# A transformer trunk on one core: transposed input loaded, a quarter of one modulation on TensorE, and a new order of the first loads

## The chip, the cores and the metric

The kernel runs on one core of a Trainium2 chip. The metric is the device time of one execution in microseconds. Three runs of the kernel before took 1611.92, 1613.42 and 1616.47 us; their median is 1613.42 us. The engines of the core are TensorE (PE in the profile; PEld are its weight loads), VectorE (DVE), ScalarE (ACT), GpSimd (POOL) and SyncE (SP), which here only issues transfers. All arithmetic is in 32 bits.

## The reference

One encoder layer over 256 tokens of width D = 2048, with a condition vector c that modulates it:

```python
cond = silu(c)
sh1, sc1, g1, sh2, sc2, g2 = split(cond @ ada_w + ada_b, 6)      # 2048 each
h = rmsnorm(x, norm1_g) * (1 + sc1) + sh1
x = x + g1 * mixer(h)       # q, k, v, u = split(h @ w_in); neighbourhood attention of 16 heads,
                            # a 2-D Fourier mix of u, a sigmoid gate per branch (h @ w_bg), output projection
h = rmsnorm(x, norm2_g) * (1 + sc2) + sh2
x = x + g2 * hier_moe(h)    # one of 4 groups, then 2 of its 8 SwiGLU experts, per token
out = rmsnorm(x, final_g)
```

The weights of all 32 experts (2 MB tiles, 403 MB in all) are read whatever the routing; with the other weights some 611 MB come from memory in each execution. The change concerns sh1 and sc1 (shift 1 and scale 1), the normalised x that they are applied to, and the first products with w_in and w_bg.

## The kernel before

**Layout.** The modulated input h is kept transposed: 16 chunks of 128 channels (on the partitions) by 256 tokens, each as a sum of a high part `hh` and a low part `hl` in a rounded 32-bit type. A *pair* is two neighbouring chunks; there are 8 pairs. Every weight tile is [128, 1024] (512 KB). `load` (L100) takes the next of `NW` = 8 buffers in turn and issues the transfer on SP's queue, which therefore holds the tiles in the order of the program and stops where a buffer is not free yet. `split_w` (L110) makes the high part of a weight tile on ScalarE (L107) and the low part on VectorE (L108). `t_part` and `n_part` multiply one weight tile (512 output columns, two chunks) in 24 matmuls of 256 columns, or 12 of 512: high by high, high by low, low by high.

**The start.** ScalarE's queue brings c, the constant table, a table of vectors and x (tokens on the partitions, two tiles of 1 MB). The silu of c is made twice: as `condR`, its row broadcast to all partitions by matmuls with a row of ones (L190 to L197), and as `condT`, transposed (L198 to L201). The sums of squares of x are made on ScalarE (L339), `rstd_of` makes the reciprocal root, VectorE scales x (L342), TensorE transposes it in 32 pieces (L348), and ScalarE and VectorE copy them to `xT` (L350).

**Shift 1 and scale 1.** `ada1_some(n)` (L238) takes the next n of 64 weight tiles, eight for each pair. Each holds, for 128 output channels on the partitions, half of the 2048 inputs along the row. `dot` (L213) multiplies it by `condR` on VectorE and sums along the row. After the eighth, `h_pair` (L247) makes shift and scale (`modulation`, L225), applies them to two chunks of `xT` (VectorE L252, ScalarE L253), and splits the result into `hh` and `hl`.

**The first loop (L356 to L379).** Its four passes p = 0 to 3 cover the 16 chunks, four chunks (two pairs) in a pass, for nine sections of 512 output columns, listed in `first`: u twice, q, k, v and four gate sections. A pass has 18 loads, two per section (s = 0 needs the first pair, s = 1 the second). The two u sections (si < 2) keep their sums in PSUM over all passes; the others are evicted at the end of each pass: by ScalarE (L377) in pass 0, by VectorE as an addition to the tile in SBUF (L379) later. In a pass the loads of the first four sections are ordered s = 0 of all four, then s = 1; the five others follow one by one. After each load, `want` says how many of the 64 tiles of shift 1 and scale 1 are to have been used by then; `LEAD` = 3 sets them ahead. When none is left, `ada_some(1)` starts on the tiles of the other modulations (128 tiles in all, multiplied and accumulated on VectorE, L223, `mac`), one for each load, also in all later sections up to the output projection; there `PACE` gives 14 more, and the rest are taken after it.

**Order.** The program is written in this order, and a planner that works on modelled times orders the instructions of each engine, with the program's order as priority. `keep_in_program_order`, which the change uses, pins an instruction behind the instruction that the program wrote last on the same engine.

**After the loop** come the Fourier mix, attention, the branch projections, the output projection, routing, and from about 680 us on the experts, whose weights stream through SP's queue.

Of the kernel before, what the change touches and what calls it, by code (L numbers as in the profile page):

```python
# [15 lines left out]
P = 128  # L16
# [41 lines left out]
def build(tc, A, out, dbg=None):  # L58
# [106 lines left out]
    c16 = cp.tile([16, P], F32, name="c16")  # L165
# [7 lines left out]
    nc.scalar.dma_start(c16, A["c"])  # L173
# [15 lines left out]

    condR = xp.tile([P, D], F32, name="condR")  # L190
    for i in range(2):
        crow = wp.tile([P, 1024], F32, tag="w", name=nm("crow"))
        nc.sync.dma_start(crow[0:1, :], A["c"].rearrange("a b -> (a b)")[None, 1024 * i:1024 * i + 1024])
        for j in range(2):
            ps = acc.tile([P, 512], F32, tag="acc", name=nm("pc"))
            mm(ps, ones[0:1, :], crow[0:1, 512 * j:512 * j + 512], True, True)
            nc.scalar.activation(condR[:, 1024 * i + 512 * j:1024 * i + 512 * j + 512], ps, AF.Silu)  # L197
    nc.scalar.activation(c16, c16, AF.Silu)  # L198
    pt = mps()
    nc.tensor.transpose(pt[:, :16], c16, ident[:16, :16])  # L200
    nc.vector.tensor_copy(condT, pt[:, :16])  # L201
# [23 lines left out]
    def modulation(dst, parts, k, vs, vc, vn):  # L225

        bi = [vecT[:, v + k.start:v + k.stop] for v in (vs, vc, vn)]
        nc.vector.tensor_tensor(dst, parts[:, :, :, 0], parts[:, :, :, 1], op=OP.add)
        nc.vector.tensor_tensor(dst[:, 0], dst[:, 0], bi[0], op=OP.add)
        nc.vector.scalar_tensor_tensor(dst[:, 1], dst[:, 1], 1.0, bi[1], op0=OP.add, op1=OP.add)  # L230
        nc.vector.tensor_tensor(dst[:, 1], dst[:, 1], bi[2], op=OP.mult)

# [14 lines left out]
    def h_pair(pr):  # L247
# [3 lines left out]
        hf = s4([P, 2, T], "hf")  # L251
        nc.vector.tensor_scalar(hf[:, 0, :], xT[:, 2 * pr, :], ab[:, 1, 0:1], ab[:, 0, 0:1], op0=OP.mult, op1=OP.add)  # L252
# [83 lines left out]
    xT = xp.tile([P, KC, T], F32, name="xT")  # L336
    xTv = xT.rearrange("p k t -> p (k t)")
# [5 lines left out]
    for k2 in range(8):  # L343
        px = acc.tile([P, 512], F32, tag="acc", name=nm("px"))
        for i in range(2):
            for tb in range(2):
                kc = 2 * k2 + i
                nc.tensor.transpose(px[:, T * i + P * tb:T * i + P * tb + P], xt[tb][:, kc * P:kc * P + P], ident)  # L348
        pv = px.rearrange("p (a b) -> p a b", a=2)
# [3 lines left out]
    at_u, mp_u = att.tile([P, 2, 512], F32, tag="s", name="at_u"), [mps(), mps()]  # L353
    fixed = [[x.rearrange("p (a b) -> p a b", a=2) for x in v] for v in ((at_u[:, 0], at_u[:, 1]), mp_u)]
# [635 lines left out]
```

## Time and profile before

| | |
|---|---|
| median of three runs | 1613.42 us |
| the profiled execution's own time | 1614.69 us |
| its span (first to last instruction) | 1612.9 us |
| busy: PE, DVE, ACT, POOL | 1236.5, 680.5, 349.5, 45.1 us |
| bytes moved, mean rate | 616.27 MB, 382 GB/s |
| mean granted clock of TensorE | 0.901 |

The profile comes from one execution. Busy time is a sum over instructions of an engine; matmuls are pipelined, so that a busy TensorE need not be at its peak. A wait is put down to what ended last of those things that an instruction waited for. The chain of waits follows the work that ended last back from the end. A few per cent of the matmul records can be missing.

### The profile page before, as it was taken

To read this page: it belongs to the slowest core of one execution; us is meant where nothing else is said; L and a number is where in the kernel's file an instruction comes from. 1 tells how busy PE (TensorE), PEld (TensorE's weight loads), DVE (VectorE), ACT (ScalarE), POOL (GpSimd) and SP (SyncE) were. 2 spreads that over 40 slices of the span, in tenths; PEclk is the share of its full clock that TensorE was granted. 3 is DMA by queue.
4 is the path that set the end of the run, shared out by engine and by line. 5 is a ranking of instruction groups with operands and counts; after the bars stand their busy time and mean duration, and the time that the engine had idled before them with its cause. 6 is when DMAs were issued, how large, how long until landed. Compare 5 with 4: busy or idle time off the path is not lost.

```text
span 1612.9 us, 20394 instructions
## 1 busy us (share of the span) xinstructions
PE 1236.5 (77%) x8430; PEld 749.7 (46%) x8430; DVE 680.5 (42%) x946; ACT 349.5 (22%) x535; POOL 45.1 (3%) x40
## 2 busy tenths in 40 slices
PE   5999999999999869798658558558568567555765
PEld 3989899898899746544103113113113012111111
DVE  6989999788887936712002002002003002002002
ACT  4543355444545324211001001000000000000001
POOL 0000000300001100000000000000000000000001
PEclk9999999999999989899789889889859779778878
DMA  9999999899997997699999999999999999999996
GB/s 361 388 334 348 352 341 363 277 327 376 315 352 259 337 407 265 245 402 427 427 426 426 427 427 427 426 427 427 427 427 426 427 428 427 417 426 427 424 427 283
DMA packets 89228, 616.27 MB, mean 382 GB/s; under 512 B 10036, under 2 KB 10340, under 8 KB 64936
## 3 DMA queue, kind: packets, MB, share of 16 engines
q1 hardware_dynamic: 87700, 611.10, 94.5%
q10 hardware_dynamic: 1252, 3.48, 0.6%
q8 instruction: 68, 1.11, 0.3%
q0 software_dynamic: 176, 0.31, 0.1%
q14 instruction: 32, 0.26, 0.0%
HBM read 611.71 MB, written 2.10 MB: 381 GB/s over the span
## 4 chain that ended last, share of the span: by engine, by line
DMA 48%; PE 32%; DVE 6%; issue 2%; ACT 1%; DVEq 0%; ACTq 0%; SPq 0%
DMA w<-exw 43%; PE acc L116 16%; DMA w<-ada 3%; PE ph L116 3%; PE pu L116 3%; PE pg L116 3%; PE pd L116 3%; DVE lo L108 2%; PE m L116 2%; DVE ada L223 2%; DMA w<-mow 1%; PE po L116 1%; PE pr L116 1%; ACT hq L755 0%; DMA w<-mixw 0%
## 5 line engine op out<-in xcount | busy, mean ns | idle before, releaser
L116 PE MATMUL pg<-w,hq 128*32 128x512 f32 x1024 | 179.9, 754 | 222.6 <-DMA w<-exw 222.6
L108 DVE TENSOR_TENSOR lo<-w,hi 128x1024 fp32r<-128x1024 f32 x192 | 239.4, 1251 | 45.4 <-ACT hi L107 39.3
L107 ACT CAST hi<-w 128x1024 fp32r<-128x1024 f32 x192 | 200.7, 1050 | 246.3 <-PE acc L116 170.7
L788 DVE TENSOR_TENSOR act<-act,pu 128x512 f32<-128x512 f32 x8 | 5.5, 688 | 524.0 <-PE pu L116 524.0
L116 PE MATMUL acc<-hh,hi 128*128 128x256 f32 x768 | 211.2, 279 | 0.6 <-ACT hi L107 0.6
L116 PE MATMUL acc<-hl,hi 128*128 128x256 f32 x768 | 210.5, 277 | 0.0
L116 PE MATMUL acc<-hh,lo 128*128 128x256 f32 x768 | 205.1, 278 | 3.0 <-DVE lo L108 3.0
L116 PEld LDWEIGHTS pg<-w,hq 128*32 128x32 f32 x1024 | 24.6, 116 | 364.5 <-DMA w<-exw 345.7
L116 PE MATMUL pu<-w,hq 128*32 128x512 f32 x1024 | 187.6, 782 | 0.0
L223 DVE SCALAR_TENSOR_TENSOR ada<-w,condT,ada 128x1024 f32<-128x1024 f32 x124 | 163.4, 1323 | 34.1 <-DMA w<-ada 33.1
L116 PE MATMUL pd<-w,aT 128*32 128x512 f32 x1024 | 137.7, 656 | 31.9 <-DMA w<-exw 31.0
L784 ACT ACTIVATE act<-pg 128x512 f32<-128x512 f32 x8 | 4.8, 597 | 653.5 <-PE pg L116 653.5
L116 PEld LDWEIGHTS acc<-hh,hi 128*128 128x128 f32 x768 | 144.5, 188 | 2.1 <-ACT hi L107 1.4
L116 PEld LDWEIGHTS acc<-hl,hi 128*128 128x128 f32 x768 | 144.3, 188 | 0.3 <-issue 0.2
L116 PEld LDWEIGHTS acc<-hh,lo 128*128 128x128 f32 x768 | 140.6, 188 | 4.0 <-DVE lo L108 3.6
L116 PE MATMUL po<-yb,gwt 128*128 128x512 f32 (+1 forms) x132 | 72.4, 637 | 32.0 <-DVE yb L806 21.0
L116 PEld LDWEIGHTS pu<-w,hq 128*32 128x32 f32 x1024 | 42.1, 135 | 105.4 <-issue 104.3
L116 PEld LDWEIGHTS ph<-gt,x 128*128 128x128 f32 x512 | 67.9, 200 | 46.9 <-issue 22.7
L116 PEld LDWEIGHTS pd<-w,aT 128*32 128x32 f32 x1024 | 29.6, 115 | 115.2 <-issue 61.1
L116 PE MATMUL ph<-gt,x 128*128 128x128 f32 x512 | 78.1, 295 | 5.8 <-ACT hq L755 3.8
L215 DVE SCALAR_TENSOR_TENSOR w<-w,condR 128x1024 f32<-128x1024 f32 x64 | 77.6, 1217 | 10.7 <-ACT condR L197 7.4
L813 DVE TENSOR_TENSOR x<-x,po 128x512 f32<-128x512 f32 (+1 forms) x66 | 44.3, 671 | 84.8 <-PE po L116 84.7
(246 smaller groups left out, 1489.1 us busy)
## 6 DMA issues: line engine op xcount, KB each, us to landing
w<-exw SPq DMA_DIRECT2D x186, 2048.0 KB, 30.8
w<-ada SPq DMA_DIRECT2D x192, 512.0 KB, 5.5
w<-mixw SPq DMA_DIRECT2D x64, 512.0 KB, 5.6
w<-gatew SPq DMA_DIRECT2D x64, 512.0 KB, 5.4
w<-mow SPq DMA_DIRECT2D x32, 512.0 KB, 5.7
w<-exw SPq DMA_DIRECT2D x24, 512.0 KB, 11.0
w<-fow SPq DMA_DIRECT2D x16, 512.0 KB, 5.8
w<-now SPq DMA_DIRECT2D x16, 512.0 KB, 5.0
```

The lines of the kernel that those rows point to most:

```text
L107: nc.scalar.copy(hi, src)
L108: nc.vector.tensor_tensor(lo, src, hi.bitcast(F32), op=OP.subtract)
L116: return nc.tensor.matmul(ps, lhsT, rhs, start=start, stop=stop, skip_group_check=True)
L215: nc.vector.scalar_tensor_tensor(w, w, 1.0, condR[:, 1024 * kh:1024 * kh + 1024], op0=OP.mult, op1=OP.mult, accum_out=dst)
L223: nc.vector.scalar_tensor_tensor(a, w, condT[:, kc:kc + 1], a, op0=OP.mult, op1=OP.add)
L784: nc.scalar.activation(at_[:, 0], pg, AF.Silu)
L788: nc.vector.tensor_tensor(at_[:, 1], at_[:, 0], pu, op=OP.mult)
L813: nc.vector.tensor_tensor(x2[:, tb, c], base[:, tb, c], po[:, 0:n], op=OP.add)
```

## The change

x also comes transposed from memory (`xT`, in four parts), and is no longer scaled and transposed on the chip. The reciprocal root of each token is broadcast to all partitions as `rB` (a diagonal times ones on TensorE), and each pair of chunks is multiplied by it in `h_pair`. For pairs 0 and 1, shift 1 and scale 1 are computed on TensorE: their 16 weight tiles come in another layout (inputs on the partitions), `condM` holds each value of `condT` 32 times as stationary operand, and eight matmuls of 32 rows by 128 columns for each tile accumulate in PSUM; a copy and a transpose bring the result to the partitions. Pairs 2 to 7 use the dot products as before. `condR` is now a broadcast transfer and a silu over it. The first loads are ordered anew. In a pass the first group is three sections instead of four; only section 0 stays in PSUM, section 1 is evicted in each pass like the others. `want` grows by three instead of two in the first loads.

```diff
+    xt = [a8("xt") for _ in range(2)]
+    for tb in range(2):
+        (nc.sync, nc.scalar)[tb].dma_start(xt[tb], A["x"][:, tb, :])
+    nc.scalar.dma_start(condT, A["cT"])
     nc.scalar.dma_start(cst, A["cst"])
     nc.scalar.dma_start(vec, A["vec"])
-    xt = [a8("xt") for _ in range(2)]
-    for tb in range(2):
-        nc.scalar.dma_start(xt[tb], A["x"][:, tb, :])
...
+    nc.scalar.dma_start(xT[:, 0:4], A["xT"][:, 0:4])
+    nc.scalar.activation(condT, condT, AF.Silu)
+    nc.vector.tensor_copy(condM, condT[:, :, None].to_broadcast([P, KC, 32]))
...
     def ada1_some(n):
         for _ in range(min(n, len(ada1_q))):
             pr, i, u, kh = ada1_q.pop(0)
+            if pr < 2:
+                k4 = 4 * i + 2 * u + kh
+                w = load(A["ada1p"][pr, k4])
+                if k4 == 0:
+                    ada1_parts[pr] = mps()
+                pa = ada1_parts[pr]
+                for kj in range(2):
+                    for j in range(4):
+                        mm(pa[32 * j:32 * j + 32, 0:P], condM[:, 2 * k4 + kj, :],
+                           w[:, 512 * kj + P * j:512 * kj + P * j + P], k4 == 0 and kj == 0, k4 == 7 and kj == 1)
+                if k4 == 7:
+                    t = s4([P, P], "ca")
+                    nc.scalar.copy(t, pa[:, 0:P])
+                    pt = mps()
+                    nc.tensor.transpose(pt[:, 0:P], t, ident)
+                    ada1_parts[pr] = pt[:, 0:P].rearrange("p (u i r) -> p u i r", u=2, i=2)[:, :, :, 0]
+                    h_pair(pr)
+                continue
...
         hf = s4([P, 2, T], "hf")
+        nc.vector.tensor_tensor(xT[:, k, :], xT[:, k, :], rB[:, None, :].to_broadcast([P, 2, T]), op=OP.mult)
...
-        nc.scalar.activation(xTv[:, tb * D:tb * D + D], xt[tb], AF.Square, accum_out=ss1[:, tb:tb + 1])
-    rs1 = rstd_of(xp, ss1, 2)
-    for tb in range(2):
-        nc.vector.tensor_scalar(xt[tb], xt[tb], rs1[:, tb:tb + 1], None, op0=OP.mult)
...
-                nc.tensor.transpose(px[:, T * i + P * tb:T * i + P * tb + P], xt[tb][:, kc * P:kc * P + P], ident)
...
-        (nc.scalar.copy if k2 % 2 else nc.vector.tensor_copy)(xT[:, 2 * k2:2 * k2 + 2, :], pv)
+    nc.scalar.activation(xt[0], xt[0], AF.Square, accum_out=ss1[:, 0:1])
+    nc.vector.scalar_tensor_tensor(xt[1], xt[1], 1.0, xt[1], op0=OP.mult, op1=OP.mult, accum_out=ss1[:, 1:2])
+    rs1 = rstd_of(xp, ss1, 2)
+    rB = xp.tile([P, T], F32, name="rB")
+    pr_ = att.tile([P, 512], F32, tag="s", name="prb")
+    for tb in range(2):
+        dg = s4([P, P], "dg")
+        nc.vector.tensor_scalar(dg, ident, rs1[:, tb:tb + 1], None, op0=OP.mult)
+        mm(pr_[:, P * tb:P * tb + P], ones, dg, True, True)
+    nc.scalar.copy(rB, pr_[:, 0:T])
...
-        order = [(si, s) for s in range(2) for si in range(4)] + [(si, s) for si in range(4, 9) for s in range(2)]
+        order = [(si, s) for s in range(2) for si in range(3)] + [(si, s) for si in range(3, 9) for s in range(2)]
...
-                opened[si] = fixed[si] if si < 2 else acc_tiles()
+                opened[si] = fixed if si == 0 else acc_tiles()
...
-            want = 8 + 2 * count if count <= 4 else 16 + (count - 4 + LEAD) * 16 // 18
+            if count == 3:
+                for i in (4, 8):
+                    tc.keep_in_program_order(nc.sync.dma_start(xT[:, i:2 * i], A["xT"][:, i:2 * i]))
+                    if i == 4:
+                        tc.keep_in_program_order(nc.sync.dma_start(condR, A["crow"].to_broadcast([P, D])))
+                nc.scalar.activation(condR, condR, AF.Silu)
+            want = 8 + 3 * count if count <= 2 else 16 + (count - 3 + LEAD) * 16 // 18
...
-                if p == 0 or si < 2:
+                if p == 0 or si == 0:
                     nc.scalar.activation(o, i, AF.Copy, scale=scale)
```

## Rows read from the trace of the kernel before

**Rows 1.** The page's chain of waits, shares of the span by line.

```profile
DMA w<-exw 43%; PE acc L116 16%; DMA w<-ada 3%; PE ph L116 3%; PE pu L116 3%; PE pg L116 3%; PE pd L116 3%; DVE lo L108 2%; PE m L116 2%; DVE ada L223 2%; DMA w<-mow 1%; PE po L116 1%; PE pr L116 1%; ACT hq L755 0%; DMA w<-mixw 0%
```

**Rows 2.** Stretches: length, busy of PE, PEld, DVE, ACT, POOL, clock, DMA share, GB/s.

```profile
86.80:140.40 53.60, 51.06 (x414) 49.46 (x413) 49.27 (x71) 21.06 (x23) 0.00 (x0) 1.00 0.94 337
140.40:194.40 54.00, 51.42 (x423) 49.82 (x422) 52.10 (x82) 20.80 (x22) 0.00 (x0) 1.00 0.94 341
194.40:252.00 57.60, 54.99 (x448) 52.99 (x448) 55.35 (x61) 33.50 (x47) 0.00 (x0) 0.97 0.96 350
252.00:550.00 298.00, 291.79 (x2489) 272.73 (x2488) 258.26 (x261) 138.59 (x220) 33.01 (x25) 1.00 0.90 324
...
700.00:1612.90 912.90, 600.54 (x3645) 179.51 (x3636) 108.97 (x220) 48.65 (x104) 7.52 (x6) 0.85 0.99 420
```

**Rows 3.** The same view for stretches of the start.

```profile
2.50:30.00 27.50, 14.04 (x42) 8.50 (x42) 17.77 (x37) 11.53 (x16) 0.04 (x1) 1.00 1.02 406
30.00:35.00 5.00, 1.02 (x3) 0.73 (x3) 4.86 (x9) 3.75 (x6) 0.00 (x0) 0.65 0.94 330
35.00:40.00 5.00, 4.85 (x29) 4.54 (x29) 5.00 (x8) 0.58 (x2) 0.00 (x0) 0.67 0.94 306
40.00:48.90 8.90, 8.18 (x72) 7.89 (x70) 8.83 (x19) 5.00 (x6) 0.00 (x0) 1.00 1.02 396
48.90:86.80 37.90, 37.90 (x309) 36.92 (x310) 33.88 (x52) 20.56 (x27) 0.00 (x0) 1.00 1.01 387
```

**Rows 4.** Instructions in order of time at the start: start, us, engine, line, tiles.

```profile
8.34 1.23 DVE L215 SCALAR_TENSOR_TENSOR w<-w,condR 128x1024 f32<-128x1024 f32 x1 [7.38 <-ACT condR L197]
...
33.62 0.58 PE L116 MATMUL at_u<-hh,hi 128*128 128x256 f32 x1 [4.07 <-ACT hh L107]
...
47.50 0.28 PE L116 MATMUL at_u<-hh,hi 128*128 128x256 f32 x1
...
48.89 0.39 PE L116 MATMUL at_u<-hl,hi 128*128 128x256 f32 x1 [0.72 <-DVE hl L108]
```

**Rows 5.** ScalarE in order of time, the last eviction of pass 0.

```profile
87.03 0.60 ACT L377 ACTIVATE m<-acc 128x512 f32<-128x512 f32 x1 [0.76 <-PE acc L116]
```

**Rows 6.** ScalarE in order of time, where pair 7 is made.

```profile
195.89 0.60 ACT L253 ACTIVATE hf<-xT,ab 128x256 f32<-128x256 f32 x1 [7.68 <-DVE ab L231]
196.40 1.03 ACT L107 CAST hi<-w 128x1024 fp32r<-128x1024 f32 x1
197.39 0.62 ACT L107 CAST hh<-hf 128x512 fp32r<-128x512 f32 x1
```

**Rows 7.** Single kinds of instruction by line and tile, from several views.

```profile
L215 DVE SCALAR_TENSOR_TENSOR w<-w,condR x64: 1210/1217/1227, 8.3 to 188.2; 128x1024 f32<-128x1024 f32 x64
L203 PE MATMUL m<-cst,vec 128*128 128x128 f32 x1 | 0.5, 474 | 0.0
L204 DVE COPY vecT<-m 128x128 f32<-128x128 f32 x1 | 0.3, 287 | 0.0
L231 DVE TENSOR_TENSOR ab<-ab,vecT x8: 150/158/161, 31.2 to 195.6; 128x2 f32<-128x2 f32 x8
L379 DVE SCALAR_TENSOR_TENSOR m<-acc,m x24: 677/682/692, 123.8 to 251.9; 128x512 f32<-128x512 f32 x24
129.61 1.28 DVE L379 SCALAR_TENSOR_TENSOR m<-acc,m 128x512 f32<-128x512 f32 x2
L108 DVE TENSOR_TENSOR hl<-hf,hh x8: 680/684/686, 35.3 to 198.6; 128x512 fp32r<-128x512 f32 x8
```

**Rows 8.** Transfers by issue: count, size, median us from issue to landing.

```profile
w<-mixw SPq DMA_DIRECT2D x64, 512.0 KB, 5.6
```

**Rows 9.** The chain after 684 us: start, us, what, count of matmuls.

```profile
684.24 0.99 PE pg L116 x8
685.24 0.86 PE pu L116 x8
```

**Rows 10.** The chain behind the output projection: start, us, what.

```profile
660.04 1.28 DVE ada L223
```

More of the change, by code (lines that the diff above doesn't have):

```diff
@@ L164, in build @@
     cst = cp.tile([P, C_END], F32, name="cst")
-    c16 = cp.tile([16, P], F32, name="c16")
     vec = cp.tile([P, P], F32, name="vec")
@@ L188, in build @@
     xp, _xp = pool("xp")
+    xT = xp.tile([P, KC, T], F32, name="xT")
+    condM = xp.tile([P, KC, 32], F32, name="condM")
     condR = xp.tile([P, D], F32, name="condR")
[L191 to L201, printed above, removed]
+    nc.scalar.dma_start(xT[:, 0:4], A["xT"][:, 0:4])
+    nc.scalar.activation(condT, condT, AF.Silu)
+    nc.vector.tensor_copy(condM, condT[:, :, None].to_broadcast([P, KC, 32]))
     pt = mps()
@@ L227, in modulation @@
         bi = [vecT[:, v + k.start:v + k.stop] for v in (vs, vc, vn)]
[L228 to L230 removed]
+        if len(parts.shape) == 4:
+            nc.vector.tensor_tensor(dst, parts[:, :, :, 0], parts[:, :, :, 1], op=OP.add)
+            parts = dst
+        nc.vector.tensor_tensor(dst[:, 0], parts[:, 0], bi[0], op=OP.add)
+        nc.vector.scalar_tensor_tensor(dst[:, 1], parts[:, 1], 1.0, bi[1], op0=OP.add, op1=OP.add)
         nc.vector.tensor_tensor(dst[:, 1], dst[:, 1], bi[2], op=OP.mult)
@@ L240, in ada1_some @@
             pr, i, u, kh = ada1_q.pop(0)
+            if pr < 2:
[16 more added lines that the diff above has]
+                continue
             if (i, u, kh) == (0, 0, 0):
                 ada1_parts[pr] = xp.tile([P, 2, 2, 2], F32, tag="ap", bufs=2, name=nm("ap"))
-            dot(load(A["ada1"][u, 2 * pr + i, kh]), ada1_parts[pr][:, u, i, kh:kh + 1], kh)
+            dot(load(A["ada1"][u, 2 * pr + i - 4, kh]), ada1_parts[pr][:, u, i, kh:kh + 1], kh)
             if (i, u, kh) == (1, 1, 1):
@@ L335, in build @@
     ss1 = xp.tile([P, 2], F32, name="ss1")
[L336 to L350 removed]
+    nc.scalar.activation(xt[0], xt[0], AF.Square, accum_out=ss1[:, 0:1])
[3 more added lines that the diff above has]
+    pr_ = att.tile([P, 512], F32, tag="s", name="prb")
+    for tb in range(2):
+        dg = s4([P, P], "dg")
+        nc.vector.tensor_scalar(dg, ident, rs1[:, tb:tb + 1], None, op0=OP.mult)
+        mm(pr_[:, P * tb:P * tb + P], ones, dg, True, True)
+    nc.scalar.copy(rB, pr_[:, 0:T])
     ada1_some(8)
[L353 to L354 removed]
+    at_u = att.tile([P, 2, 512], F32, tag="s", name="at_u")
+    fixed = [at_u[:, i].rearrange("p (a b) -> p a b", a=2) for i in range(2)]
     count = 0
     for p in range(4):
[L357 removed]
+        order = [(si, s) for s in range(2) for si in range(3)] + [(si, s) for si in range(3, 9) for s in range(2)]
         opened = {}
@@ L931, in arrays_of @@
     a["x"] = c(x.transpose(1, 0, 2))
-    a["c"] = c(g["c"].reshape(16, P))
+    a["xT"] = c(x.reshape(T, KC, P).transpose(2, 1, 0))
+    a["cT"] = c(g["c"].reshape(16, P).T)
+    a["crow"] = c(g["c"].reshape(1, D))
     a["cst"] = const_table()
@@ L935, in arrays_of @@
     ada = g["ada_w"][0]
-    a["ada1"] = c(ada[:, :2 * D].reshape(2, 1024, 2, 16, P).transpose(2, 3, 0, 4, 1))
+    a["ada1"] = c(ada[:, :2 * D].reshape(2, 1024, 2, 16, P).transpose(2, 3, 0, 4, 1)[:, 4:])
+    a["ada1p"] = c(ada[:, :2 * D].reshape(8, 2, P, 2, 8, 2, P)[:, :, :, :, 0:2].transpose(4, 0, 2, 1, 3, 5, 6)
+                   .reshape(2, 8, P, 1024))
     a["ada2"] = c(ada[:, 2 * D:].reshape(16, P, 4, 2, 1024).transpose(2, 0, 3, 1, 4))
```

3 lines of the change are left out of this document (1 added, 2 removed).

## The prediction

> **What bounds the kernel now.** I read the chain of waits first. It lies mostly on the transfers of the expert weights [rows 1], but these are the second half of the program. The busy times by stretch say where each engine limits [rows 2]: from 700 us on the transfers run at 420 GB/s with a busy share of 0.99, so that part has a fixed length; from 252 to 550 us TensorE is busy 292 of 298 us. Neither stretch is touched, and each starts when the one before it ends. So I take every microsecond won or lost before 252 us as one of the end, and the question is when the four passes p = 0 to 3 of the first loop end.
>
> At the start VectorE is late: its first dot product waits 7.38 us for the broadcast condition, the first real projection matmul comes at 33.62 us, and the granted clock in the two stretches after that is 0.65 and 0.67, with TensorE busy for only 1.02 of the 5 us before 35 us [rows 3, 4]. The matmuls of the four loads that need only pair 0 end at 47.50 us; the first one on the second half of pair 1 starts at 48.89 us [rows 4]. From there to the last eviction of pass 0 at 87.03 us [rows 5] TensorE has no gap [rows 3]. With a few records missing I count by the program: 14 loads x 24 matmuls = 336 in 38.0 us, 0.113 us each. So pass 0 is bound by TensorE after a start that VectorE sets.
>
> A pass holds 18 loads x 24 = 432 matmuls, 48.8 us at that pace. Passes 1 to 3 take 53.6, 54.0 and 57.6 us, with VectorE busy for 49.3, 52.1 and 55.4 us [rows 2]. There ScalarE waits for VectorE's shift and scale, 7.68 us in the worst of three such places [rows 6]. So those passes are near VectorE's limit, and a load more on it counts there.
>
> **The change, part by part.** *What goes at the start.* 16 of 64 dot products (1.22 us each [rows 7], 19.5 us of VectorE), the scaling of x, the 32 transposes and their copies. All of it ends before 35 us or stands in VectorE's backlog of pass 0. What is late next are the transfers, since the sixteen weight tiles are still read, and more than before.
>
> *When the first matmuls can run.* Bytes in the order of the queues, from shapes (a weight tile is 0.524 MB [rows 8]): x 2.10, tables 0.32, the router's weights 0.30, the first quarter of the transposed x 0.52, pair 0 in eight tiles 4.19: 7.44 MB. At the 406 GB/s of 2.5 to 30 us [rows 3] that is 20.8 us. A copy (0.29), a transpose (0.47), three small operations (0.16 each), hf (0.60) and its rounding (0.62) [rows 6, 7], with some gaps, put the first projection matmul near 24 us, 9.6 us before today's 33.62.
>
> *What then stops it.* Only three loads now stand before pair 1 is needed (four before). Behind the third load the queue of SP gets 2.62 MB: 12 of the 16 chunks of transposed x, and the condition row broadcast to 128 partitions (1.05). The last two tiles of pair 1, two dot tiles and load 4 come behind these. In cumulative MB: load 1 7.96, load 3 12.15, the end of the 2.62 MB 14.78, pair 1 complete 15.82, load 4 17.40. At 406 GB/s load 3 lands at 32.4, pair 1 at 41.5 and load 4 at 45.4 us. The three loads' matmuls (8.1 us) and pair 1's work end near 39 us, so TensorE waits. After 41.5 us the small chain above leads to 45 us, after 45.4 us the rounding of load 4 (1.05, nearest row 1.03 [rows 6]) and its low half (1.22; nearest the dot of the same size [rows 7]) to 47.7 us. Behind that waiting chain stand ScalarE's roundings of loads 4 and on, which nobody can use sooner.
>
> The added matmuls of pair 1 (8 tiles x 8) aren't in the trace. Eight of the same 32-column kind on 512 columns take 0.86 us [rows 9], so on 128 columns a tile costs 0.21 us; if each weight load set the pace, as slow as those eight, 0.86. I take 0.5, 4 us in all, beside the wait: no cost, and at most 2 us without that cover. The switch between kinds shows as 0.99 against 0.86 us [rows 9]. The Trainium skill (TensorEngine Tiling (Array Packing), Key Properties) says that a change of tiling mode drains TensorE; the trace agrees with about 0.13 us, 2 us for 16 switches, in the same idle time, so the sum is the same by either.
>
> A clock that falls in that wait costs what it cost today, up to 2 us (about a third of the 5 us of 35 to 40 us [rows 3]); below that nothing. I take 1, since TensorE does some work in the gap. Load 4 then counts as started at 48.7 us. 15 loads of 24 matmuls at 0.113 us are 40.7 us: pass 0 ends at 89.4 against about 86.9 us, **+2.5**. Bounds: 0 (420 GB/s, the best row [rows 2], and no clock loss) and +5.7 (355 GB/s from 30 us on, the mean of 30 to 48.9 us [rows 3], and the full clock loss).
>
> The Trainium skill (DMA: Bandwidth & Descriptors, Queues, rings and completion order) speaks against a gain by new order: the queues of SP and ACT have rings on the same 16 DMA engines, which take turns. The trace agrees: 1.02 busy with both queues in use.
>
> *Passes 1 to 3.* Section 1 leaves its own PSUM tile and is evicted in each pass: two more on VectorE in passes 1 to 3 (0.68 us alone, 0.60 behind another: two take 1.28 [rows 7]). The multiplication by rB comes with each pair; nearest row hl, same size, 0.68, 0.60 pipelined. So pass 1 gets 4 x 0.60 = 2.4 us. Pass 2 gets 2.4 and a first accumulate (0.7, called an estimate between an eviction and a dot): 3.1. Pass 3 gets two evictions (1.2) and loses a dot (1.2) and pair 7, which is complete one load sooner (about 1.5): -1.5. Pass 1 has 4.3 us without VectorE work and can hide most: +0.5 (bounds 0, 2.4). Pass 2 has 1.9: +3.1 (1.2, 3.1). Pass 3: -1.5 (-6, if the 7.68 us wait nearly goes; +1.2). Together **+2.1**.
>
> *Later.* The second table of modulations starts one load earlier, so 7 instead of 8 of its tiles remain behind the output projection. One accumulate of 1.28 us is on the chain there [rows 10]: **-1.2** (bounds -2.4, 0). The condition's Silu over 2048 columns waits on ScalarE for a transfer that ends at 36.3 us; its user, the first dot, has its tile after 41.5 us: nothing.
>
> Sum: +2.5 + 2.1 - 1.2 = +3.4 on the profiled execution's 1614.69 us (span 1612.9 and 1.8 around it): 1618.1. The median shown is 1.3 us lower, so 1616.8: **1617 us**. A difference below 0.3% (4.8 us) counts as none.
>
> **Rivals.**
> *Slower by the transfers.* The 2.62 MB behind load 3 and the denser reading after it run at 355 instead of 406 GB/s. Load 4 is 2.2 us later, the clock loses its full 2, and 15 pairs of a load and a dot tile take 2.95 instead of 2.71 us each (+3.6): +6.8, 1624 us. It decides when load 4 lands after 47 us. For it: 306 to 330 GB/s around 35 us. Against: the queue was starved of free buffers there, and 406 before.
> *Slower by VectorE.* Nothing of the added work hides in passes 1 to 3: +2.4 + 3.1 + 1.2 instead of 2.1, 1621.5 us. For it: those passes' busy shares of 0.92 to 0.96. Against: the gaps in pass 1.
> *Faster by shorter waits.* Pair 7 complete in pass 2 takes pass 3's long wait away (-6 instead of -1.5) and pass 0 ends even: 1610 us, less with the full -2.4 behind. Against: its lead over its first use stays four loads.
> *Faster because the queue is ordered otherwise.* If the planner puts the 2.62 MB behind load 4, it lands at (17.40 - 2.62) MB, 38.9 us, and pass 0 ends 6.5 us earlier than forecast, 1610 us; with the clock kept up and 420 GB/s 1608. Then the change would not keep its written order. Against: these issues wait for nothing, and follow load 3.
>
> **How the numbers follow.** Forecast 0.46 (1611 to 1623: 0.01 faster, 0.35 same, 0.10 slower); transfers 0.14, all slower; VectorE 0.16 (0.13 slower, 0.03 same); shorter waits 0.14 (0.09 faster, 0.05 same); other order 0.10 (0.07 faster, 0.03 same). Faster 0.17, same 0.46, slower 0.37. The range 1607 to 1626 holds these cases and the bounds (-5 and +10 us together).
>
> **What would show it.** Right: the first projection matmul near 24 us, a TensorE gap from about 39 to 46 us, load 4's matmuls at 46 to 48 us, pass 0 ending near 89 us, VectorE busier in passes 1 and 2. Wrong: load 4 before 44 us, no gap, pass 0 before 85 us; or passes 1 to 3 shorter than 165 us together.

## The result: 1.8% slower, and the profile after

The changed kernel takes 1643.84 us (median of four runs, 1642.32 to 1644.89), the kernel before took 1612.87 us beside it. The ratio is 1.0181, with a 95% interval of 1.0164 to 1.0198: 29 us slower (31 by the two medians), where 4 were forecast. Where a difference below is said to be by the ratios, it is a difference of such ratios times 1614 us, good to some 3 or 4 us; marks in a trace are those of one execution.

The loss stands mainly in two places, pass 0 and the stretch from pass 2's end to the output projection. A table of marks, read off the trace of one execution each (us: first projection matmul, last eviction of passes 0, 2 and 3, first matmul of the output projection, first expert matmul, span):

```
             first   p0     p2     p3    output  expert   span
before        33.6   87.0  193.7  251.9   537.1   684.2  1612.9
after         28.8   96.1  203.8  267.6   564.3   711.2  1640.5
difference    -4.9   +9.1  +10.1  +15.7   +27.2   +27.0   +27.6
```

The page's chain of waits after, which answers to [rows 1]: more of it is transfers of the small weights, less is TensorE.

```profile
DMA w<-exw 47%; PE acc L116 14%; DMA w<-ada 5%; DVE lo L108 3%; PE pg L116 3%; PE pd L116 2%; PE ph L116 2%; PE pu L116 2%; DMA w<-gatew 2%; DMA w<-mixw 2%; DVE ada L217 2%; PE m L116 2%; PE at_u L116 1%; DVE w L209 1%; DMA condR<-crow 1%
```

The stretches that answer to [rows 2, 3] (length, busy of PE, PEld, DVE, ACT, POOL, clock, DMA share, GB/s): the start, passes 1 to 3, the sections up to the output projection, and the experts.

```profile
2.50:30.00 27.50, 9.25 (x183) 7.32 (x183) 8.32 (x20) 8.96 (x12) 0.04 (x1) 0.96 0.97 377
...
40.00:45.00 5.00, 2.50 (x41) 2.03 (x44) 2.50 (x4) 1.49 (x1) 0.00 (x0) 1.00 1.02 410
45.00:50.00 5.00, 0.85 (x13) 0.22 (x5) 3.39 (x9) 2.33 (x4) 0.00 (x0) 0.51 1.02 408
50.00:55.00 5.00, 3.44 (x14) 3.15 (x15) 5.00 (x8) 2.19 (x3) 0.00 (x0) 0.50 1.03 410
...
60.00:65.00 5.00, 5.00 (x46) 5.00 (x45) 3.76 (x5) 2.82 (x5) 0.00 (x0) 1.00 1.03 410
...
75.00:80.00 5.00, 5.00 (x47) 5.00 (x46) 4.08 (x6) 2.71 (x4) 0.00 (x0) 1.00 1.01 391
...
85.00:90.00 5.00, 5.00 (x47) 5.00 (x46) 2.96 (x6) 2.46 (x4) 0.00 (x0) 1.00 0.94 342
...
96.10:148.50 52.40, 50.57 (x406) 48.62 (x406) 49.87 (x77) 18.14 (x20) 0.00 (x0) 1.00 0.94 339
148.50:203.80 55.30, 52.43 (x408) 51.02 (x408) 52.67 (x80) 20.88 (x22) 0.00 (x0) 0.94 0.94 338
203.80:267.60 63.80, 57.65 (x460) 54.27 (x461) 60.48 (x66) 33.03 (x44) 0.00 (x0) 1.00 0.94 336
267.60:564.30 296.70, 284.29 (x2418) 265.96 (x2418) 243.46 (x243) 134.33 (x216) 32.37 (x24) 0.99 0.89 308
711.20:1640.50 929.30, 611.60 (x3763) 181.62 (x3762) 110.88 (x225) 51.85 (x111) 7.50 (x6) 0.86 0.99 418
```

The experts take 929 us as before. Pass 0 ends 9.1 us later: TensorE does little from 42 to 52 us while the transfers run at 408 to 410 GB/s, and its granted clock falls to 0.51, the lower of its two levels, and stays there until 55 us. From 55 to 90 us TensorE is busy without a gap. From pass 2's end to the output projection 17.1 us are lost, in stretches where the change touches no line but the loop's; there the transfers run slower than before (308 GB/s against 324 to 325) although nothing is moved that was not moved before.

ScalarE's and TensorE's instructions that answer to [rows 4, 5], in order of time (in brackets the idle time ahead and what ended it):

```profile
9.87 1.28 ACT L352 ACT_TABLE_LOAD   x1 [9.87 <-DMA xt<-x]
...
13.19 1.28 ACT L194 ACT_TABLE_LOAD   x1
14.48 0.22 ACT L194 ACTIVATE condT<-condT 128x16 f32<-128x16 f32 x1
14.71 1.28 ACT L151 ACT_TABLE_LOAD   x1
...
18.84 0.37 ACT L362 COPY rB<-prb 128x256 f32<-128x256 f32 x1 [2.62 <-PE prb L116]
...
18.94 1.30 PE L116 MATMUL m<-w,condM 128*32 128x128 f32 x20
...
28.76 0.58 PE L116 MATMUL at_u<-hh,hi 128*128 128x256 f32 x1
...
44.66 0.72 PE L116 MATMUL m<-w,condM 128*32 128x128 f32 x16 [0.64 <-DMA w<-ada1p]
...
48.54 1.04 ACT L107 CAST hi<-w 128x1024 fp32r<-128x1024 f32 x1 [0.31 <-DMA w<-mixw]
...
50.15 0.58 PE L116 MATMUL at_u<-hh,hi 128*128 128x256 f32 x1 [3.94 <-ACT hh L107]
...
51.04 1.04 ACT L107 CAST hi<-w 128x1024 fp32r<-128x1024 f32 x1 [0.94 <-DMA w<-mixw]
...
52.14 0.79 PE L116 MATMUL acc<-hh,hi 128*128 128x256 f32 x2 [1.41 <-ACT hi L107]
...
54.73 0.41 PE L116 MATMUL at_u<-hl,hi 128*128 128x256 f32 x1
54.94 0.41 PE L116 MATMUL at_u<-hh,lo 128*128 128x256 f32 x1
...
55.60 0.29 PE L116 MATMUL at_u<-hh,hi 128*128 128x256 f32 x1
55.72 0.28 PE L116 MATMUL at_u<-hl,hi 128*128 128x256 f32 x1
...
62.04 0.60 ACT L395 ACTIVATE q<-acc 128x512 f32<-128x512 f32 x1 [0.76 <-PE acc L116]
...
96.10 0.60 ACT L395 ACTIVATE m<-acc 128x512 f32<-128x512 f32 x1
```

Three loads of activation tables at 1.28 us each make ScalarE's chain long, the broadcast of the reciprocal root (`prb`) stands ahead of pair 0's matmuls on TensorE, and these begin at 18.94 us. Pair 1's last tile comes at 44.66, load 4's high half is made at 48.54, load 5's at 51.04, and the first matmul on pair 1 starts at 50.15. At 62.04 the third section is evicted, so that six of pass 0's 18 loads are done. Between 57 and 95 us no idle time of TensorE or ScalarE ends with the landing of a weight tile, and one of VectorE does, 0.3 us.

**Where the sections lose.** VectorE between 205 and 540 us, by line (count, busy, mean ns, idle time ahead and its releasers). Before:

```profile
L108 DVE TENSOR_TENSOR lo<-w,hi 128x1024 fp32r<-128x1024 f32 x102 | 130.3, 1280 | 21.8 <-ACT hi L107 17.4 <-issue 4.2
L223 DVE SCALAR_TENSOR_TENSOR ada<-w,condT,ada 128x1024 f32<-128x1024 f32 x96 | 125.7, 1313 | 14.4 <-DMA w<-ada 13.4
```

After:

```profile
L108 DVE TENSOR_TENSOR lo<-w,hi 128x1024 fp32r<-128x1024 f32 x100 | 122.9, 1233 | 13.4 <-ACT hi L107 13.2
L217 DVE SCALAR_TENSOR_TENSOR ada<-w,condT,ada 128x1024 f32<-128x1024 f32 x90 | 119.9, 1333 | 42.5 <-DMA w<-ada 41.9
```

VectorE waits three times as long for the tiles of the second table, 41.9 against 13.4 us. Two tiles in pass 3 of the changed kernel show how, by their issues on SP, the high half on ScalarE and their uses on VectorE:

```profile
207.74 0.33 SPq L103 DMA_DIRECT2D w<-mixw  x1
...
218.28 0.33 SPq L103 DMA_DIRECT2D w<-ada  x1
...
219.00 1.05 ACT L107 CAST hi<-w 128x1024 fp32r<-128x1024 f32 x1 [2.25 <-PE at_u L116]
...
222.69 1.28 DVE L217 SCALAR_TENSOR_TENSOR ada<-w,condT,ada 128x1024 f32<-128x1024 f32 x1 [0.24 <-DMA w<-ada]
223.89 1.22 DVE L108 TENSOR_TENSOR lo<-w,hi 128x1024 fp32r<-128x1024 f32 x1
```

Counted through SP's queue, the tile issued at 218.28 is accumulated at 222.69, as it lands, and the one issued 10.5 us earlier, at 207.74, has its high half at 219.00 and its low half only behind that accumulate, at 223.89. The accumulate stands ahead of a low half whose tile is seven places older in the queue, and VectorE works in order: it sat idle for 0.24 us ahead of the accumulate, although the high half that the low half needs was done at 220.05. The Trainium skill (PSUM — Partial Sum Buffer, Engine vs sequencer instructions) calls the queues of ScalarE, VectorE and GpSimd strict FIFO; this trace agrees. The old tile keeps one of the 8 buffers meanwhile, so the next transfer starts later. The planner chose this order; the mean distance in places (accumulate's tile behind the tile of the next low half) and the mean time from issue to use are:

```
                    pass 2   pass 3   later   low half / accumulate used after issue, later
before                2.8      1.7     5.3      17.0 / 6.4 us
after                 5.0      5.7     6.8      19.1 / 5.6 us
```

"Later" is the stretch behind the loop up to the pause in the accumulates near its end (after 497 us before, after 518 in the changed kernel). In pass 2 the "accumulates" are the dot products.

### The profile page after: what moved, and what is told of

Read it like the earlier page. It is cut to its first block, busy times and chain, and to the rows that moved or that the text cites. A ratio compares the mean times of both kernels' runs of the same rounds, so it can differ in the third digit from the quotient of the medians.

```text
span 1640.5 us, 20849 instructions
## 1 busy us (share of the span) xinstructions
PE 1241.2 (76%) x8651; PEld 753.6 (46%) x8651; DVE 668.4 (41%) x924; ACT 348.4 (21%) x531; POOL 50.4 (3%) x40
## 4 chain that ended last, share of the span: by engine, by line
DMA 58%; PE 28%; DVE 9%; issue 2%; ACT 2%; POOL 0%; DVEq 0%; SPq 0%; ACTq 0%; POOLq 0%
DMA w<-exw 47%; PE acc L116 14%; DMA w<-ada 5%; DVE lo L108 3%; PE pg L116 3%; PE pd L116 2%; PE ph L116 2%; PE pu L116 2%; DMA w<-gatew 2%; DMA w<-mixw 2%; DVE ada L217 2%; PE m L116 2%; PE at_u L116 1%; DVE w L209 1%; DMA condR<-crow 1%
## 5 line engine op out<-in xcount | busy, mean ns | idle before, releaser
L108 DVE TENSOR_TENSOR lo<-w,hi 128x1024 fp32r<-128x1024 f32 x192 | 234.6, 1227 | 47.1 <-ACT hi L107 46.0
L116 PE MATMUL acc<-hh,hi 128*128 128x256 f32 x832 | 231.3, 281 | 4.9 <-ACT hi L107 4.3
L116 PE MATMUL acc<-hl,hi 128*128 128x256 f32 x832 | 230.2, 279 | 0.0
L116 PE MATMUL acc<-hh,lo 128*128 128x256 f32 x832 | 225.5, 280 | 1.0 <-DVE lo L108 0.8
L217 DVE SCALAR_TENSOR_TENSOR ada<-w,condT,ada 128x1024 f32<-128x1024 f32 x124 | 167.3, 1352 | 66.3 <-DMA w<-ada 65.6
L116 PEld LDWEIGHTS acc<-hh,hi 128*128 128x128 f32 x832 | 157.6, 190 | 7.5 <-ACT hi L107 5.7
L116 PEld LDWEIGHTS acc<-hl,hi 128*128 128x128 f32 x832 | 157.6, 189 | 0.5 <-issue 0.3
L116 PEld LDWEIGHTS acc<-hh,lo 128*128 128x128 f32 x832 | 153.9, 189 | 3.0 <-DVE lo L108 1.9
L824 DVE TENSOR_TENSOR yb<-pd,g2r 128x512 f32<-128x512 f32 (+1 forms) x33 | 22.2, 675 | 126.8 <-PE pd L116 126.8
```

Of the source, the lines that this page charges most:

```text
L108: nc.vector.tensor_tensor(lo, src, hi.bitcast(F32), op=OP.subtract)
L116: return nc.tensor.matmul(ps, lhsT, rhs, start=start, stop=stop, skip_group_check=True)
L217: nc.vector.scalar_tensor_tensor(a, w, condT[:, kc:kc + 1], a, op0=OP.mult, op1=OP.add)
L824: nc.vector.tensor_tensor(yb[:, l], pd[:, l], g2r[:, c], op=OP.mult)
```

## The experiments

"Pinned" means: an accumulate (or dot product) is put behind the low half of a named load on VectorE, and the planner may not move it ahead. Each kernel ran in three rounds beside the kernel before; the ratio is against that.

**Later sections pinned: b_pin0, a_pin0, b_pin1, a_pin1.** The kernel before (b) and the changed one (a), with the accumulates of the sections after the loop directly behind the low half of their own load (0) or one load later (1).

```diff
             i = mac(a[:, 1024 * hf:1024 * hf + 1024], w, kc, kc == 0 and part in (1, 2))
+            if pin[0]:
+                tc.add_manual_dep(i.ins, wlow[-1].ins.name, ...)   # no semaphore, order alone
```

> The kernel before, with one thing pinned: from the gate section after the first loop up to the output projection VectorE takes strictly in turn the low half of a load and the accumulate of the tile behind it (low, accumulate, low, accumulate), the order that the changed kernel's planner chose. Theory A (order): the 12 us that the change loses between the end of pass 3 and the first matmul of the output projection (285 us before, 297 us after) come from this order alone, so this kernel loses them too: that stretch 293 to 300 us, end 1621 to 1628 us. Rival B (lead lost at the start): the weight transfers lose their lead over TensorE in the first 50 us and never get it back, whatever the order; then this kernel, whose start is the old one, stays at 285 us, end 1611 to 1616 us.

> The changed kernel with the same pin (low, accumulate, in turn). Its own order is nearly this already. Theory A and rival B both expect the stretch from the end of pass 3 to the first matmul of the output projection within 4 us of the changed kernel's 297 us, end 1638 to 1646 us; if A holds it stands beside the pinned kernel before with a difference of about 15 us, what the first loop lost.

> The kernel before with each accumulate pinned behind the low half of the next load (low 1, low 2, accumulate 1, low 3, accumulate 2), in the same sections. Theory A: a load's low half goes ahead of the accumulate, so TensorE's work is made first: the stretch after the first loop 283 to 288 us, end 1611 to 1617 us. Rival B: the same, as the start is the old one.

> The changed kernel with each accumulate pinned behind the low half of the next load. Theory A: the stretch after the first loop falls from 297 to 284 to 289 us, end 1626 to 1632 us, some 15 us above the kernel before. Rival B: the lead is lost at the start, order doesn't give it back: 294 to 300 us and 1638 to 1646 us.

Measured: b_pin0 1614.52 us (ratio 0.9984, 0.9967 to 1.0000), a_pin0 1631.56 (1.0088, 1.0059 to 1.0116), b_pin1 1619.59 (1.0025, 1.0009 to 1.0041), a_pin1 1629.47 (1.0079, 1.0054 to 1.0105). The stretch from pass 3's end to the output projection: 285.7, 288.5, 289.6, 287.6 us (before 285.1, after 296.7). Plain alternation is not the cause, since b_pin0 alternates and loses nothing; that expectation failed. b_pin1 missed too, at 289.6 us and 1619.59. But a pin of either kind takes 15 to 17 us from the changed kernel by the ratios, and 8 to 9 us from this stretch (296.7), so this part of the loss is one of order, not of a lead lost at the start. It was after these runs that I counted places. (The letters: here A is the order as such and B a lead lost at the start; in the later texts C is the order on VectorE and B the bytes.)

**Everything pinned: a_pinall, and the order forced the other way: b_ahead3.** a_pinall pins the dot products of passes 1 to 3 and the accumulates of pass 3 too. b_ahead3 is the kernel before with the accumulates put ahead; to get them there, the weight tiles are also issued three loads ahead of their use:

```diff
-            f(load(src[s]), acs, a, b, 2 * s, s == 0, s == n - 1)
-            ada_some(ada)
+            f(tile_of(), acs, a, b, 2 * s, s == 0, s == n - 1)   # loaded 3 loads ahead, each with its
+                                                                 # accumulate; the low half pinned behind the latest
```

> The changed kernel with every accumulate of the second table (in the sections and in pass 3) and every dot product of passes 1 to 3 put behind the low half of the load before it on VectorE; nothing else is changed. Theory C, order on VectorE: in the changed kernel the accumulates run 5.7 places of SP's queue ahead of the low halves in pass 3 (1.7 in the kernel before), so VectorE waits for transfers while older tiles wait for it; with the order mended pass 3 takes 58 to 60 us (63.8 in the changed kernel, 61.9 with the order mended in the later sections alone), pass 2 54 us, the stretch from the end of pass 3 to the first output projection stays at 286 to 289, and the time is 1622 to 1626 us. Rival D, the loop's own reorganisation (section 1 evicted in each pass) costs the time of pass 3: pass 3 stays at 62 to 64 us and the time at 1628 to 1631.

> The kernel before with the accumulates put ahead: from pass 3 on the weight tiles are issued three loads before their use, each with the tile of the second table behind it, and each low half is put behind the accumulate of three loads later on VectorE (7 places of SP's queue ahead; 1.7 in pass 3 and 4 to 8 after it in the kernel before). Nothing of the change is in it. Theory C: pass 3 takes 62 to 64 us (58.2), the stretch from its end to the first output projection 293 to 299 (285.2), the time 1624 to 1632. Rival E, VectorE's order is not the cause and the changed kernel loses its time in those stretches by something else: pass 3 under 60, the stretch under 289, the time 1611 to 1619.

a_pinall: 1629.04 us (1.0075, 1.0052 to 1.0097); b_ahead3: 1644.97 us (1.0186, 1.0151 to 1.0222). VectorE in b_ahead3, same view and stretch as above:

```profile
L229 DVE SCALAR_TENSOR_TENSOR ada<-w,condT,ada 128x1024 f32<-128x1024 f32 x91 | 119.6, 1314 | 55.7 <-DMA w<-ada 47.6 <-DMA ada<-ada_b_row 7.7
L110 DVE TENSOR_TENSOR lo<-w,hi 128x1024 fp32r<-128x1024 f32 x93 | 114.7, 1238 | 0.0
```

And in a_pinall, where the wait is gone:

```profile
L230 DVE SCALAR_TENSOR_TENSOR ada<-w,condT,ada 128x1024 f32<-128x1024 f32 x96 | 129.5, 1352 | 0.0
L110 DVE TENSOR_TENSOR lo<-w,hi 128x1024 fp32r<-128x1024 f32 x102 | 127.4, 1249 | 23.3 <-ACT hi L109 22.3
```

The kernel before, with nothing of the change but accumulates that run ahead (7.2 places in pass 3, 7.6 later) and the earlier issue, is as slow as the changed kernel, and slower there than expected: pass 3 took 65.5 us, the stretch behind it 318.7, a loss of 33.6 where the changed kernel loses 11.6. So it shows that the two edits together cost this much, not that the order alone does. a_pinall missed: its time lies in rival D's range, and pass 3 stayed at 61.8 us, near the rival's 62. From pass 2's end to the first expert matmul it took 494.5 us (507.4 after, 490.5 before), of which the stretch up to the output projection gave back 10.0 and pass 3 2.0 us.

**The distance: b_ahead2.** As b_ahead3 with two loads.

> The run b_ahead3 with the tiles issued two loads before their use instead of three, so that the accumulates stand 5 places of SP's queue ahead of the low halves instead of 7. Theory C, order on VectorE, with the 8 buffers as its measure: at 5 places the tiles that wait for their low half hold fewer buffers and VectorE meets landed tiles, so most of the loss of b_ahead3 (1645.0) is gone: pass 3 takes 58 to 61 us (65.5), the time is 1614 to 1624. Rival G, not the distance but the issue of the section's tiles ahead of the attention's small transfers costs the time: 1635 or more.

1635.86 us (1.0104, 1.0087 to 1.0121): a miss. The counted distance was 5.3 places in pass 3, and that pass took 59.0 us (58.3 before, 65.5 at 7.2 places), as expected; but in the later sections the planner ran further ahead by itself, 6.8 places, and that stretch took 317.6 us, about what b_ahead3 took at 7.6 places. The changed kernel, at the same 6.8 places, takes 296.7. So the mean distance doesn't tell the cost there, and the time is what rival G forecast (1635 or more); that the earlier issue costs most of the later loss in b_ahead2 and b_ahead3 isn't excluded. Only pass 3 tells 5 places from 7, and the changed kernel's pass 3 fits it badly: 63.8 us at 5.7 places, and still 61.8 with the order mended.

**The bytes: a_late_pinall, a_fix_pinall, a_nobytes_pinall.** Three edits to a_pinall: the 2.62 MB behind load 5; that and a mended start; the 2.62 MB left out.

```diff
-            if count == 3:
+            if count == 5:
...
-    ada1_some(8)
+    ada1_some(7)      # the sums of squares and rB stand between
+    ada1_some(1)
```

> The run a_pinall with the 2.62 MB (twelve chunks of transposed x, the broadcast condition) issued behind load 5 instead of load 3, and the dot products that need them from load 6 on. Theory P, place: load 4 lands near 45 us (51.0 in the changed kernel), TensorE's gap before it shrinks to under 4 us, pass 0 ends at 90 to 91 us (96 to 97) and the time is 5 to 7 us under that of a_pinall, 1616 to 1620. Rival B, bytes: pass 0 ends when the bytes for it have been moved, and these are the same: pass 0 ends at 95 to 97, the time is that of a_pinall within 2 us.

> The run a_late_pinall with the start mended: the condition is the first transfer of ScalarE's queue and its silu the first activation, and the broadcast of the reciprocal root is written behind seven of pair 0's eight tiles. Theory P and a blocked start: pair 0's matmuls start at 13 to 15 us (18.9), load 1 is issued 3 to 4 us earlier, the transfers of 2.5 to 30 us run at 400 GB/s or more (377), pass 0 ends at 87 to 89 us and the time is 2 to 4 us under that of a_late_pinall, 1613 to 1617. Rival B, bytes: only the 0.6 MB more that are moved at the start count, 1.5 us.

> The run a_pinall without the 2.62 MB behind load 3: the dot products read a constant in place of the condition, and all pairs of chunks are made from the first four chunks of x, so the values are others; instructions and waits are the same but for these transfers and one silu. Theory B, bytes: 2.62 MB at 390 GB/s are 6.7 us: pass 0 ends at 89 to 91 us (96.9 in a_pinall), the time is 1621 to 1624 (1629). Rival S, the late end of pass 0 comes from the start (blocked first tiles, the clock, the chain of pair 1): pass 0 ends at 94 or later and the time is 1626 or more.

a_late_pinall 1624.31 us (1.0051, 1.0033 to 1.0069), pass 0 ends at 95.8 us; a_fix_pinall 1623.78 (1.0052, 1.0038 to 1.0066), 94.8; a_nobytes_pinall 1619.11 (1.0016, 1.0003 to 1.0029), 90.8 (96.9 in a_pinall). (The 51.0 us of the first expectation are load 5's; load 4's high half was made at 48.54.) In a_late_pinall the high halves of loads 4 and 5 are made at 44.77 and 46.23 us, and still pass 0 ends only 1.1 us earlier, for TensorE's clock is low for ten us and it waits between 55 and 60 us (same columns as the stretches above):

```profile
45.00:50.00 5.00, 3.26 (x13) 2.97 (x14) 5.00 (x8) 4.97 (x5) 0.00 (x0) 0.60 1.02 410
50.00:55.00 5.00, 5.00 (x34) 5.00 (x33) 4.75 (x9) 2.03 (x3) 0.00 (x0) 0.72 1.02 406
55.00:60.00 5.00, 3.42 (x30) 3.22 (x28) 3.41 (x6) 2.74 (x5) 0.00 (x0) 1.00 1.03 406
```

The instructions around that wait, on TensorE and on ScalarE:

```profile
46.37 0.58 PE L121 MATMUL at_u<-hh,hi 128*128 128x256 f32 x1 [2.60 <-ACT hh L109]
...
58.46 0.60 ACT L429 ACTIVATE q<-acc 128x512 f32<-128x512 f32 x1 [0.58 <-PE acc L121]
58.95 3.04 ACT L109 CAST hi<-w 128x1024 fp32r<-128x1024 f32 x3
...
60.04 0.38 PE L121 MATMUL acc<-hh,hi 128*128 128x256 f32 x1 [1.62 <-ACT hi L109]
```

The high half that TensorE waits for stands on ScalarE behind evictions that wait for TensorE. Three high halves follow without a gap, and between 57 and 95 us none of the waits that the profile lists for TensorE, ScalarE and VectorE ends with a transfer. So the bytes don't bind this part of pass 0, although the transfers run at a share of 1.02 up to 60 us: the 3.8 us that TensorE starts earlier on pair 1 (46.37 instead of 50.15) go in low clock and in waits for ScalarE and VectorE. Taking the 2.62 MB out, which also brings load 4 forward (its high half is made at 42.98 us, 48.31 in a_pinall), gave 6.1 us at pass 0's end (6.7 expected) and 9.5 of the time. Since a_late_pinall won only 1.1 us there, the place of the bytes isn't all that counts; that the bytes count wherever they stand isn't shown either. The time of a_late_pinall lies between the two theories, 3.9 us under a_pinall by the ratios; 2.8 of them were won in passes 1 and 2, after the end that I had taken as the measure. a_fix_pinall's start did what it should (first projection matmul at 26.6 us, 403 GB/s from 2.5 to 30) and won nothing in the time.

**Bytes in the kernel before: b_pinall, b_bytes_pinall.** The kernel before pinned, and with three transfers more:

```diff
+            if count == 4:
+                for i in range(3):
+                    tc.keep_in_program_order(nc.sync.dma_start(extra[:, 1024 * i:1024 * i + 1024], ...))
```

> The kernel before with all accumulates and the dot products of passes 1 to 3 put behind the low half of the load before them on VectorE; the base of the next run. Theory C, order on VectorE: the kernel before has little to win from it, since its accumulates run only 2 to 5 places ahead where it is not yet starved: pass 0 ends at 87 us, the stretch from pass 2's end to the first output projection takes 343 to 347 us (343.4 before), the time is 1612 to 1618.

> The run b_pinall with three more transfers of 0.524 MB behind load 4, into tiles that nobody reads; no other work is added. Theory B, bytes: pass 0 ends when its bytes have been moved, so 1.57 MB at the 390 GB/s of pass 0 put its end 4.0 us later, 90.5 to 92 us, and the time 4 us above that of b_pinall. Rival T, pass 0 is bound by TensorE after load 4, as predicted: pass 0 ends within 1 us of that of b_pinall, and so does the time within 1.5.

b_pinall 1612.30 us (0.9965, 0.9950 to 0.9979), b_bytes_pinall 1614.76 (1.0000, 0.9985 to 1.0014). b_pinall's time is as expected, its stretch from pass 2's end to the output projection is not: 348.9 us, with 137.7 instead of 147.1 behind it up to the experts. So its gain is not one in the sections. Pass 0 ends at 88.4 and 89.1 us, where rival T had it and the bytes theory did not. But the time of b_bytes_pinall is 5.6 us above that of b_pinall by the ratios (2.5 by the medians), nearer to the bytes theory's 4 than to the rival's 1.5, and the traces don't show where: the traced execution of b_pinall is its slowest, that of b_bytes_pinall among its fastest. The stretch where they went, in b_pinall and then in b_bytes_pinall:

```profile
30.00:45.00 15.00, 10.71 (x67) 10.11 (x68) 14.80 (x27) 5.67 (x8) 0.00 (x0) 0.77 0.94 334
```

```profile
30.00:45.00 15.00, 10.82 (x68) 10.23 (x69) 13.70 (x26) 5.93 (x8) 0.00 (x0) 0.77 1.03 408
```

74 GB/s more over 15 us are 1.1 of the 1.57 MB. In the kernel before the share of the transfers is 0.94 there, and more bytes fill the hole. The changed kernel has no such hole. So pass 0's end hardly moves when bytes are added into a hole; whether they are free in the time isn't shown.

**The loop alone: b_loop_pinall.** b_pinall with the changed kernel's three sections in the first group and section 1 evicted in each pass.

> The run b_pinall with the changed kernel's loop: three sections in the first group, section 1 evicted in each pass, the tiles of pair 1 asked for in two steps of three instead of four of two; its start, its dot products and its bytes are those of the kernel before. Theory L, the loop costs what the prediction's sum said, +2.1 us over passes 1 to 3 and nothing after: the time is 1613 to 1616 (1612.3 in b_pinall). Rival F, the loop is free: within 1 us of b_pinall in passes 1 to 3 and in the time. Rival H, the loop costs what is left between a_nobytes_pinall and b_pinall (1619.1 against 1612.3): 1617 to 1621.

1617.58 us (0.9996, 0.9985 to 1.0008). By the ratios it is 5 us slower than b_pinall, by the marks 2.3 over passes 1 to 3 and 1.9 in the span; the traced execution of b_pinall is 3.3 us above its median. Between theory L (2.1) and rival H (5 or more) I can't decide. Pass 3 takes 57.7 us (57.0 in b_pinall), so the loop alone isn't what makes it long in a_pinall.

**Two versions that failed: a_lean_pinall, a_row_pinall.** Both were to read fewer bytes and give the same result.

```diff
-                        tc.keep_in_program_order(nc.sync.dma_start(condR, A["crow"].to_broadcast([P, D])))
+        mm(ps, ones[0:1, :], crow[i // 2][0:1, ...], True, True)      # four times, then the silu
...
+                        if pr == 1 and kj + j == 0:
+                            tc.keep_in_program_order(i_)              # pair 1 behind load 1
```

> The run a_pinall with all that the change adds to the transfers taken out, and the same result: x is read only transposed (2.10 MB at the start, none later), its sum of squares comes from squares of that and two matmuls with ones, and the condition is broadcast by matmuls from a row of 8 KB, as in the kernel before; the condition's silu is the first activation. 3.15 MB less. Theory B, bytes: pass 0 ends at 86 to 89 us (96.9), the time is 1617 to 1621. Rival S: pass 0 ends at 92 or later, since pair 1's chain and the order of the first matmuls are as they were, and the time is 1624 or more.

> The run a_fix_pinall with the broadcast condition made by four matmuls from a row of 8 KB instead of a transfer of 1.05 MB, and with the order of TensorE's first matmuls kept as written (seven tiles of pair 0, the broadcast of the reciprocal root, the eighth, load 1, then pair 1). The result is the same. Theory B, bytes: 2.62 MB less gave 9.9 us in a_nobytes_pinall, so 1.05 MB less give 3 to 4: pass 0 ends at 91 to 93 us (94.8 in a_fix_pinall), the time is 1618.5 to 1621.5. Rival S, the start and pair 1's chain hold pass 0: pass 0 ends at 94 to 96 us, the time within 1.5 us of a_fix_pinall's 1623.8.

a_lean_pinall 1636.03 us (1.0123, 1.0103 to 1.0142), a_row_pinall 1627.12 (1.0056, 1.0039 to 1.0073); pass 0 ends at 104.0 and 98.4 us. Both also kept pair 1's matmuls behind load 1's, and both starved the queue: in a_row_pinall

```profile
30.00:35.00 5.00, 5.00 (x31) 4.76 (x34) 1.23 (x1) 1.87 (x4) 0.00 (x0) 0.50 0.78 300
35.00:40.00 5.00, 5.00 (x92) 4.64 (x88) 1.23 (x1) 0.53 (x1) 0.00 (x0) 0.96 0.60 206
```

The tiles of pair 1 sat in their buffers behind matmuls that ran at a granted clock of 0.50, and few transfers could start. So these runs say nothing on bytes; that these act in proportion in a kernel with the right result is not shown.

## Why the prediction was wrong

The stretches of one execution each, in us (pass 0's end; passes 1 and 2; pass 3; from there to the output projection; from there to the experts; the span):

```
                    p0    p1, p2    p3    to output  to experts   span
before             87.0   106.7    58.3     285.1      147.1     1612.9
after              96.1   107.7    63.8     296.7      146.9     1640.5
a_pinall           96.9   108.1    61.8     286.7      146.0     1628.1
a_nobytes_pinall   90.8   109.5    57.5     287.8      146.0     1620.2
b_pinall           88.4   108.6    57.0     291.9      137.7     1613.8
```

The 29 us, by the ratios: mending the order takes 17.1 us from the changed kernel and 5.6 from the kernel before, so the order accounts for 11.5 of the difference. The other 17.7 stand between a_pinall and b_pinall: 9.5 for the 2.62 MB, 5.0 for the loop (1.9 by the marks), and a remainder of about 3 that no run assigns. This takes the parts as additive, though the bytes were taken out of the changed kernel and the loop was put into the one before. The marks agree on the order: the span falls by 12.4 us from the changed kernel to a_pinall, 10.0 of them in the stretch to the output projection, and rises by 0.9 from the kernel before to b_pinall.

*The premise failed first.* "Neither stretch is touched ... So I take every microsecond won or lost before 252 us as one of the end." The experts' part kept its length; the stretch from 252 to 550 us did not: up to the output projection it took 296.7 instead of 285.1 us, and 286.7 with the accumulates pinned. Its instructions are the same, but their order on VectorE is the planner's, made anew from the whole program. No rival had this; it is some two fifths of the loss. Why the planner chose another order, no run tells. From how many places on it costs isn't settled either: before the change the accumulates already ran 5.3 places ahead there, and pinning them won nothing there.

*"What then stops it", +2.5, was +9.1.* Here the mechanism came as forecast, and its terms were too small. The TensorE gap came (41.5 to 50 instead of 39 to 46 us), pair 1's last tile and load 4 were 3 us later than forecast (44.66 and 48.54 instead of 41.5 and 45.4). A part of that is 377 instead of 406 GB/s until 30 us, with pair 0's matmuls beginning only at 18.94 us, behind the broadcast of the reciprocal root; a_fix_pinall, where they begin at 14.6, has 403. The forecast had load 4 count as started at 48.7 us; three loads on, at 2.71 us each, that is 56.8, and the mark for it stands at 62.0. Of these 5.2 us load 4 is 3.1, and TensorE's wait for load 5's high half, which the forecast left out, is 1.4. The low clock, put at 1 us, is by estimate 1.5: from 52.1 to 55.2 us the matmuls start 0.21 us apart, afterwards 0.12. The twelve loads that were left took 34.1 instead of 32.5 us. a_late_pinall shows what the forecast lacked all the same: with load 4 early the pass ends only 1.1 us earlier, for the low clock and the order on ScalarE then stand in the way.

*The first projection matmul* came at 28.76 instead of 24 us, by the same late start of pair 0. a_fix_pinall took 2 us of that back and the time did not move.

*Passes 1 to 3, +2.1:* passes 1 and 2 together came to 107.7 us against 106.7, pass 3, forecast 1.5 us shorter, to +5.6. With the order equal the loop alone adds 2.3 us over the three (b_loop_pinall against b_pinall, 167.9 and 165.6), near the forecast. So the loop's cost was about right by the marks, but the term as a whole came to +6.6, and pass 3 is where it failed. Pinning takes 2.0 of the 5.6 off. The rest is gone in a_nobytes_pinall (57.5 us), whose pass 3 has the same loads, and stays without a cause.

*Later, -1.2:* from the output projection's first matmul to the experts' 146.9 against 147.1 us, nothing gained.

*Rivals.* "Slower by the transfers" had the nearest time, 1624 us, and its condition (load 4 after 47 us) came true, but not its cause: the rate did not fall to 355 GB/s, it was 407 to 417 from 30 to 60 us. The rule of the Trainium skill that spoke against a gain by new order (DMA: Bandwidth & Descriptors, Queues, rings and completion order) is about the queues of SP and ACT; a_late_pinall moves the bytes within SP's one queue, so no run here tests it.

The fastest version is the kernel before with its order pinned, b_pinall: 0.35% faster than the kernel before (0.21 to 0.50%), with nothing of the change in it. That is at the edge of the 0.3% that the prediction counts as none.

## What to carry to other kernels

Where a planner orders the instructions, look at engines and stretches that the change does not touch: count for each consumer how long its tile lies from issue to use, and if one kind of tile is used as it lands while an older kind waits, pin that order before judging the change. Transfers put ahead of a tile that the pass waits for cost their time: 2.62 MB, moved at a share of 1.02, cost 6.1 us at the end of pass 0. But a full queue doesn't show that a pass is bound by its bytes: look which engine the waits end on, for here from 57 us on nearly none ended with a transfer.

## What was not expected of the hardware

A section weight of 0.524 MB (`mixw` and `gatew`) took 5.1 us from issue to landing in the median of the changed kernel, but load 5, issued at 39.61 us, was used as it landed at 51.04, 11.4 us later, with the transfers at a share of 1.02. By the rates of the stretches (10.4 MB until 30 us, 4.2 until 40, then 0.41 for each us) the 17.40 MB up to load 4 were passed at 46.9 us, and it was used as it landed at 48.54. So this tile was used 1.6 us after its sum of bytes says; that tiles issued behind it are moved beside it would explain this, and no run here tests it.
